# Emitting three sequence mixers step by step between the K steps of the projections, and gating a head ahead of its norm

## The chip, the cores and the metric

The kernel runs on one core of one Trainium2 chip, as one program. The metric is the device time of an execution in microseconds (us); the numbers given are a median of three runs and one further execution that the hardware profiler recorded. The engines are TensorE (PE in the rows, its weight loads PEld), VectorE (DVE), ScalarE (ACT), GpSimd (POOL) and the queue that issues most DMAs (SP). Each engine works through its own instructions in order.

## The reference, cut to what matters

A 1024 x 1024 sequence passes through two blocks of two layers. The change touches the first block alone, whose layer is:

```
h    = rms_norm(x, pre_gain) * (1 + scale) + shift       # scale, shift, gate: mods of c
proj = h @ w_in                                          # 13 column groups
a = sliding_window_attention(aq, ak, av, sinks) * silu(ag)              # 8 heads of 64
r = rms_norm(retention(rq, rk, rv)) * silu(rg)                          # 4 heads of 64
g = rms_norm(gated_linear_attention(gq, gk, gv, log_a), gain) * silu(gg)  # 4 heads of 64
x = x + gate * rms_norm(concat(a, r, g) @ w_out, post_gain)
```

The norm of `r` and `g` is taken over each head's 64 values, so it does not matter for the result whether the product with silu comes before or after the multiplication by the norm's factor, as long as the factor is computed from the values without silu.

## The kernel before, in words

Rows (tokens) are handled in groups of four tiles of 128 (`GT = 4`), two groups (g) per layer (l), four steps in the first block. A step of `block1` does, in this order of emission: `p_attn` (products for keys and values, queries, and the attention gate, each 8 K steps), `finish` of the step before (`out_product`: the product with w_out, 2 x 8 K steps), `s_attn` (the attention mixer), `p_ret` (two products), `s_ret` (the retention mixer), `p_gla` (two products, with the norm and transposes of the next step's input between them), `s_gla` (the gated linear attention mixer). Every fp32 product is split in a high and a low part: `split_weights` makes `wh` on ACT (L201) and `wl` on DVE (L202) from each 128 x 512 weight tile, and `product` issues three matmuls (L489) per output tile and K step, 12 in a K step of four tiles, into the four PSUM banks `mm`.

What the mixers use beside `mm`: two PSUM banks `sm` for scores and transposes, and a single bank `o` for the sum over values. That bank is shared by the attention, the retention, the gated linear attention and `mods_acc.close` (L282), which reduces a chunk of the modulation vectors. Five SBUF buffers `sc` hold the mixers' temporaries. `aside` advances the modulation vectors by one chunk (8 weight tiles `aw`, DVE L310, ACT L315, POOL L316).

A retention or gated head ends in `head_norm`: ACT squares the bank `o` (L798), DVE sums the squares of each head (L800), POOL makes the factor (`rsqrt`, L207 and L208), DVE multiplies the bank by the factor (L803), POOL multiplies by the gate `sg` (L805), and `into` transposes the result on TensorE (L510) and splits it into the tiles `M` that `finish` reads. `s_gla` works in 14 levels (two halves `u` of seven block sizes `s`): POOL differences (L943, L944), ACT exponential (L945), DVE products (L947, L949), two matmuls (L954), DVE predicated copy (L957); after all 14 come the four tiles' values and norms.

What sets the order: the code is recorded by a tile framework, whose scheduler builds each engine's order by itself, by priority (order of emission, weight splits and evictions ahead) and its own cost model. A mixer emitted before a product thus does not run before it as a whole: the product's matmuls fill the places where the mixer's next instruction is not ready by that model.

Of the kernel before, what the change touches and what calls it, by code (L numbers as in the profile page):

```python
# [162 lines left out]
class Net:  # L163
    HP, HE, HX = 3000, 800, 600

    def __init__(self, ctx, tc, a):
        self.tc, self.nc, self.a = tc, tc.nc, a
        self.ctx = ctx
        self.n = 0
        self.pools = {}  # L170
# [250 lines left out]

    def split_weights(self, hi, lo, raw, g):
# [31 lines left out]
    def product(self, lhs, wsrc, nk, ncol, form, evac, gains=None, also=None):  # L454
# [18 lines left out]
        for k in range(nk):  # L473
# [8 lines left out]
            for get, w, outs, acc, flags, _ in sets:  # L482
                H, Lo = get(k)
                for j in range(outs):
                    for n, (x, y) in enumerate(((H, wh), (H, wl), (Lo, wh))):
# [5 lines left out]
                        else:  # L491
                            m = min(P, ncol - j * P)
                            nc.tensor.matmul(acc[j][:m, :w], lhsT=y[:, j * P:j * P + m], rhs=x[:, :w],  # L493
                                             start=first, stop=last)
        with self.tc.high_priority(self.HE):
# [197 lines left out]
    def s_attn(self, l, g, st, mT):  # L693
# [51 lines left out]
        def close(t):  # L745
# [11 lines left out]
            self.into(mT, 0, t, a, 4)  # L757
# [36 lines left out]

    def head_norm(self, O, sg, mT, k0, t):
        nc = self.nc
        sq = self.T("sc", [P, 256])
# [4 lines left out]
        y = self.T("sc", [P, 256])  # L802
        nc.vector.tensor_tensor(y.rearrange("p (h d) -> p h d", d=64), O[:, :256].rearrange("p (h d) -> p h d", d=64),  # L803
                                r.unsqueeze(2).to_broadcast([P, 4, 64]), ALU.mult)
        nc.gpsimd.tensor_tensor(y, y, sg, ALU.mult)  # L805
        self.into(mT, k0, t, y, 2)

    def s_ret(self, l, g, st, mT):
# [7 lines left out]
        for t in range(GT):  # L816
            tb = g * GT + t
            sc = self.T("sc", [P, 2, 2, P])
            dm = self.k1("dmask").rearrange("p (a b i) -> p a b i", a=2, b=2)
            for b in range(2):  # L820
# [4 lines left out]
                nc.vector.tensor_tensor(sc[:, :, b, :], sp, dm[:, :, b, :], ALU.mult)  # L825
            O = self.T("o", [P, 512])
            old, new = state[tb % 2], state[(tb + 1) % 2]
            if tb > 0:
                qd = self.T("sc", [P, 2, P])
                nc.vector.tensor_tensor(qd, rqk[t][:, 0:2, :], self.k1("qdec").rearrange("p (a i) -> p a i", a=2), ALU.mult)  # L830
# [15 lines left out]
            self.head_norm(O, sg[t], mT, 4, t)  # L846
            if t % 2:
                self.aside()

# [46 lines left out]
    def s_gla(self, l, g, st, mT):  # L896
# [20 lines left out]
        nc.vector.tensor_mul(kx, kx, k)  # L917
        kt = self.T("gq", [P, GT, P])
        self.transposes(kt, kx, 4)
        pr = self.T("sc", [P, 512])  # L920
        nc.vector.tensor_mul(pr, q, k)
# [5 lines left out]
        SC = []  # L927
        for u in range(2):
            us = slice(u * 256, u * 256 + 256)
            sc = self.T("st", [P, 8, P])  # L930
            SC.append(sc)
            nc.gpsimd.tensor_tensor(sc, self.k1("ident").unsqueeze(1).to_broadcast([P, 8, P]),
                                    dg[:, u * 8:u * 8 + 8].unsqueeze(2).to_broadcast([P, 8, P]), ALU.mult)
            qb = self.T("st", [P, 4, 256])
            for h in range(4):
                nc.scalar.activation(qb[:, h, :], q[:, us], AF.Copy, scale=self.k1("hsel")[:, h:h + 1])
            for n, s in enumerate((64, 32, 16, 8, 4, 2, 1)):
                v = b[:, us].rearrange("p (n two s) -> p n two s", two=2, s=s)
                nb = 256 // (2 * s)
                e = self.T("sc", [P, 256])  # L940
                ev = e.rearrange("p (n two s) -> p n two s", two=2, s=s)
                ref = v[:, :, 0, s - 1:s].to_broadcast([P, nb, s])
                nc.gpsimd.tensor_tensor(ev[:, :, 0, :], ref, v[:, :, 0, :], ALU.subtract)  # L943
                nc.gpsimd.tensor_tensor(ev[:, :, 1, :], v[:, :, 1, :], ref, ALU.subtract)  # L944
                nc.scalar.activation(e, e, AF.Exp, scale=I16)  # L945
                kl = self.T("sc", [P, 256])
                nc.vector.tensor_mul(kl, k[:, us], e)  # L947
                ql = self.T("sc", [P, 4, P])
                nc.vector.tensor_tensor(ql.rearrange("p h (n s) -> p h n s", s=s),  # L949
                                        qb.rearrange("p h (n two s) -> p h n two s", two=2, s=s)[:, :, :, 1, :],  # L950
                                        ev[:, :, 1, :].unsqueeze(1).to_broadcast([P, 4, nb, s]), ALU.mult)
                lp = self.T("sm", [P, 8, 64])
                for t in range(2):
                    nc.tensor.matmul(lp[:, t * 4:t * 4 + 4, :], lhsT=kl[:, t * P:(t + 1) * P],  # L954
                                     rhs=ql[:, :, t * 64:t * 64 + 64], start=True, stop=True)
                nbb = P // (2 * s)
                nc.vector.copy_predicated(  # L957
                    sc.rearrange("p th (n two s) -> p th n two s", two=2, s=s)[:, :, :, 1, :],
                    self.lm[:, n * 64:(n + 1) * 64].rearrange("p (n s) -> p n s", s=s).unsqueeze(1).to_broadcast([P, 8, nbb, s]),
                    lp.rearrange("p th (n s) -> p th n s", s=s))  # L960
                if n in (1, 4):
                    self.aside()
        for t in range(GT):
# [17 lines left out]
            if t % 2:  # L981
                self.aside()
# [682 lines left out]
```

## Time and profile before

| | us |
|---|---|
| median of 3 runs (lowest, highest) | 3988.06 (3983.03, 3991.77) |
| the profiled execution, its own time | 3987.53 |
| its span, first to last instruction | 3985.8 |
| TensorE busy in the span | 3756.6 (94%) |
| VectorE busy | 2432.5 (61%) |
| ScalarE busy | 1691.2 (42%) |
| GpSimd busy | 678.9 (17%) |

The first block takes roughly the first 1290 us of the span. A busy share is an average over stages; matmuls are pipelined, so a busy TensorE can still lose time between two starts, and an idle engine costs nothing where another one sets the end. The granted clock of TensorE over the span is 0.978 of full speed.

### The profile page before, as it was taken

Reading aid. Unit: us, or ns where it says so; the run is one execution under the profiler, and the core shown is the slowest. Engines: PE = TensorE matmul, PEld = TensorE weight load, DVE = VectorE, ACT = ScalarE, POOL = GpSimd, SP = SyncE. Lnnn points to the kernel's source line nnn. Section 1 sums busy time; section 2 is a strip of 40 time slices with the busy share of each in tenths; the row PEclk is TensorE's granted clock in tenths of the full one; section 3 lists DMA queues with packets and bytes.
Section 4 is the critical chain, followed back from the end, with each engine's and each line's share of the span. In section 5 each row is a group of like instructions: output and inputs, shape, how many; then the busy total and the mean of one; then the engine's idle time right before and its main releaser. Section 6 shows DMA issues by size and latency. Waiting matters only on the chain. (4 is left out here: it accounts for less than half of the span.)

```text
span 3985.8 us, 55585 instructions
## 1 busy us (share of the span) xinstructions
PE 3756.6 (94%) x19144; PEld 3068.2 (77%) x19144; DVE 2432.5 (61%) x5177; ACT 1691.2 (42%) x3652; POOL 678.9 (17%) x1058
## 2 busy tenths in 40 slices
PE   7999988998999999999999899999899999999998
PEld 5777776776777787777788788888787788887886
DVE  7677678678667657576545744344766554455444
ACT  4433344454444545455334422224544443344333
POOL 2121145235333212221001100000312100001000
PEclk9999999999999999999999999999999999999999
DMA  6234333333422412432433542222422113335332
GB/s 213 73 117 123 123 114 112 127 113 102 132 89 78 138 42 71 143 107 76 153 101 101 188 131 74 64 64 91 136 64 85 68 61 97 96 97 168 96 97 94
DMA packets 249453, 420.38 MB, mean 105 GB/s; under 512 B 32001, under 2 KB 101202, under 8 KB 249170
## 3 DMA queue, kind: packets, MB, share of 16 engines
q1 hardware_dynamic: 241426, 389.52, 31.5%
q0 software_dynamic: 7744, 27.30, 1.8%
q8 instruction: 151, 2.47, 0.3%
q14 instruction: 132, 1.08, 0.1%
HBM read 389.42 MB, written 27.30 MB: 105 GB/s over the span
## 5 line engine op out<-in xcount | busy, mean ns | idle before, releaser
L202 DVE TENSOR_TENSOR wl<-wr,wh 128x512 fp32r<-128x512 f32 (+2 forms) x948 | 640.6, 677 | 799.4 <-ACT wh L201 796.0
L201 ACT CAST wh<-wr 128x512 fp32r<-128x512 f32 (+2 forms) x948 | 554.2, 586 | 1235.8 <-PE mm L489 524.0
L489 PE MATMUL mm<-wh,M 128*128 128x512 f32 (+1 forms) x2944 | 955.3, 396 | 28.3 <-ACT M L201 17.4
L489 PE MATMUL mm<-wh,H 128*128 128x512 f32 (+2 forms) x2432 | 785.3, 396 | 7.7 <-DVE pe L640 3.6
L493 PE MATMUL mm<-H,wh 128*128 128x512 f32 x2240 | 725.6, 395 | 1.5 <-ACT wh L201 1.5
L489 PEld LDWEIGHTS mm<-wh,M 128*128 128x128 f32 x2944 | 553.0, 191 | 146.8 <-ACT M L201 25.9
L489 PE MATMUL mm<-wl,M 128*128 128x512 f32 (+1 forms) x1472 | 577.3, 392 | 0.4 <-DVE wl L202 0.4
L489 PEld LDWEIGHTS mm<-wh,H 128*128 128x128 f32 x2432 | 451.6, 194 | 95.0 <-ACT aw L315 3.3
L493 PEld LDWEIGHTS mm<-H,wh 128*128 128x128 f32 x2240 | 418.6, 189 | 80.6 <-ACT wh L201 1.8
L489 PE MATMUL mm<-wl,H 128*128 128x512 f32 (+2 forms) x1216 | 478.2, 393 | 0.0
L493 PE MATMUL mm<-H,wl 128*128 128x512 f32 x1120 | 444.1, 396 | 0.0
L489 PEld LDWEIGHTS mm<-wl,M 128*128 128x128 f32 x1472 | 281.5, 191 | 49.9 <-DVE wl L202 1.0
L489 PEld LDWEIGHTS mm<-wl,H 128*128 128x128 f32 x1216 | 235.5, 194 | 38.0 <-DVE wl L202 0.4
L493 PEld LDWEIGHTS mm<-H,wl 128*128 128x128 f32 x1120 | 211.7, 189 | 37.8
L1333 PEld LDWEIGHTS o<-kv,pT 128*128 128x128 f32 x1280 | 159.7, 193 | 28.6 <-ACT pT L1329 21.4
L1333 PE MATMUL o<-kv,pT 128*128 128x64 f32 x1280 | 169.0, 275 | 4.9 <-DVE pT L1327 2.9
L316 POOL TENSOR_TENSOR ac<-ac,aw 128x256 f32<-128x256 f32 x168 | 140.4, 836 | 157.4 <-ACT aw L315 140.5
L310 DVE SCALAR_TENSOR_TENSOR ac<-aw,c,ac 128x256 f32<-128x256 f32 x280 | 159.7, 570 | 8.3 <-DMA aw<-in_w_mod 4.4
L1418 DVE TENSOR_TENSOR Z<-Z,mm 128x512 f32<-128x512 f32 x224 | 140.1, 680 | 2.5 <-PE mm L489 2.1
L544 POOL TENSOR_TENSOR tm<-tm 128x1 f32<-128x1 f32 x34 | 7.0, 207 | 735.9 <-ACT pe L539 735.6
L1310 DVE CUSTOM_DVE_ANT_0 p<-sm,c,c 128x384 f32<-128x384 f32 (+1 forms) x144 | 82.0, 570 | 76.3 <-PE sm L1308 74.6
L1316 ACT ACTIVATE p<-p,ti 128x640 f32<-128x640 f32 (+2 forms) x144 | 110.8, 770 | 40.9 <-DVE ti L1315 38.0
(353 smaller groups left out, 5746.4 us busy)
## 6 DMA issues: line engine op xcount, KB each, us to landing
wr<-in_w_ff SPq DMA_DIRECT2D x512, 256.0 KB, 2.7
wr<-in_w_in SPq DMA_DIRECT2D x240, 256.0 KB, 2.7
wr<-in_w_out SPq DMA_DIRECT2D x144, 256.0 KB, 2.7
x<-xd SPq DMA_DIRECT2D x64, 512.0 KB, 4.9
aw<-in_w_ada SPq DMA_DIRECT2D x192, 128.0 KB, 2.1
x<-in_w_ada SPq DMA_DIRECT2D x96, 256.0 KB, 3.0
xd<-x POOLq DMA_DIRECT2D x44, 512.0 KB, 3.7
wr<-in_w_in SPq DMA_DIRECT2D x152, 128.0 KB, 2.1
```

What stands on the lines that cost most here:

```text
L201: self.nc.scalar.copy(hi, src)
L202: self.nc.vector.tensor_sub(lo, src, hi.bitcast(F32))
L310: nc.vector.scalar_tensor_tensor(acc[:, 0], wt, c[0], acc[:, 0], ALU.mult, ALU.add)
L316: nc.gpsimd.tensor_tensor(acc[:, 1], acc[:, 1], wt, ALU.add)
L489: nc.tensor.matmul(acc[j][:, :ncol], lhsT=x[:, j * P:(j + 1) * P], rhs=y[:, :ncol], start=first, stop=last)
L493: nc.tensor.matmul(acc[j][:m, :w], lhsT=y[:, j * P:j * P + m], rhs=x[:, :w], start=first, stop=last)
L544: nc.gpsimd.tensor_tensor(ss[j][:, 0:1], ss[j][:, 0:1], ss[j][:, 1:2], ALU.add)
L1310: nc.vector.tensor_tensor_reduce(sc[:, at:at + w], ps[:, :w], mask, 1.0, prev, ALU.add, ALU.max, accum_out=acc)
L1316: nc.scalar.activation(sc[:, :at], sc[:, :at], AF.Exp, bias=nm, accum_out=den[:, h:h + 1])
L1333: nc.tensor.matmul(O[:, h * 64:h * 64 + 64], lhsT=pT[:, i, :], rhs=Vs(j)[:, sl], start=i == 0, stop=i == nk - 1)
L1418: nc.vector.tensor_add(y, y, ps)
```

## The change

The three mixers become generators. `product` calls `tick` after each K step, and a tick runs the oldest generator up to its next `yield`. `s_attn` and `s_ret` are thus emitted between the K steps of `p_ret` and `p_gla`, and `s_gla` between those of the next step's `p_attn`, after which `drain` runs what is left, ahead of `finish`. Within a mixer, the scores of a unit, the values of the one before and the transposes into `M` of one still earlier are in different steps. `head_norm` multiplies the bank `o` by the gate on DVE first, and then by the factor in SBUF on DVE; POOL's gate is gone. The retention's score tile moves from `sc` to `st`. In `s_gla` the values of the first two tiles come with the tenth and the twelfth level, not after the fourteenth. `s_attn` calls `aside` twice instead of four times per step, the other mixers as often as before.

```diff
+    def tick(self):
+        while self.bg:
+            if next(self.bg[0], self) is not self:
+                return
+            self.bg.pop(0)
...
@@ product, at the end of each K step
+            self.tick()
...
@@ s_attn
-        scores(*units[0])
-        for i, (t, e) in enumerate(units):
-            if i + 1 < len(units):
-                scores(*units[i + 1])
-            values(t, e)
-            if e:
-                close(t)
-            if e:
-                self.aside()
+        ready = []
+        for i in range(len(units) + 1):
+            if i < len(units):
+                scores(*units[i])
+                yield True
+            if i:
+                values(*units[i - 1])
+                t, e = units[i - 1]
+                if e:
+                    ready.append((t, close(t)))
+                elif ready:
+                    self.into(mT, 0, ready[0][0], ready.pop(0)[1], 4)
+                yield True
+                if i % 4 == 3:
+                    self.aside()
...
@@ head_norm
+        y = self.T("sc", [P, 256])
+        nc.vector.tensor_tensor(y, O[:, :256], sg, ALU.mult)
         sq = self.T("sc", [P, 256])
         nc.scalar.activation(sq, O[:, :256], AF.Square)
...
         r = self.rsqrt(ss, 4, 4.0 / 64, 4 * EPS)
-        y = self.T("sc", [P, 256])
-        nc.vector.tensor_tensor(y.rearrange("p (h d) -> p h d", d=64), O[:, :256].rearrange("p (h d) -> p h d", d=64),
-                                r.unsqueeze(2).to_broadcast([P, 4, 64]), ALU.mult)
-        nc.gpsimd.tensor_tensor(y, y, sg, ALU.mult)
-        self.into(mT, k0, t, y, 2)
+        yh = y.rearrange("p (h d) -> p h d", d=64)
+        nc.vector.tensor_tensor(yh, yh, r.unsqueeze(2).to_broadcast([P, 4, 64]), ALU.mult)
+        return y
...
@@ s_ret
+        for i in range(GT + 2):
+            if i > 1:
+                self.into(mT, 4, i - 2, y[i - 2], 2)
+            if 0 < i <= GT:
+                y[i - 1] = values(i - 1, *sc[i - 1])
+            if i < GT:
+                sc[i] = scores(i)
+            yield True
+            if i in (2, 4):
                 self.aside()
+                yield True
...
@@ s_gla
+        for i in range(len(units) + 1):
+            if i:
+                scores(*units[i - 1], *made)
+            if i < len(units):
+                made = level(*units[i])
+            if i in (9, 11):
+                y[i // 2 - 4] = values(i // 2 - 4)
+            if i in (11, 13):
+                self.into(mT, 6, i // 2 - 5, y[i // 2 - 5], 2)
+            yield True
+            if i % 7 in (2, 5):
+                self.aside()
+        for i in range(2, GT + 2):
+            if i < GT:
+                y[i] = values(i)
+            if i > 3:
+                self.into(mT, 6, i - 2, y[i - 2], 2)
+            yield True
+            if i in (2, 4):
                 self.aside()
...
@@ block1
                 self.p_attn(l, g, hT, st, tables if n == 0 else None)
+                self.drain()
                 if pend:
                     finish(*pend)
                 mT = self.pair(GT, "M")
-                self.s_attn(l, g, st, mT)
+                self.bg.append(self.s_attn(l, g, st, mT))
                 self.p_ret(l, g, hT, st)
-                self.s_ret(l, g, st, mT)
+                self.bg.append(self.s_ret(l, g, st, mT))
...
                 self.p_gla(l, g, hT, st, ahead)
-                self.s_gla(l, g, st, mT)
+                self.bg.append(self.s_gla(l, g, st, mT))
```

How the built order changes is shown at three places; a row is a line of the program, the operation, what it writes and reads (with its buffer's number), the size, and a repetition.

The first place is TensorE at the last retention head of the second step. `o` is the bank of the head, `pu` its values, `sc` in the transposes' row (L510 before, L524 in the changed kernel) the normed and gated head, `mm` a product's bank. Before:

```order
L834 MATMUL o_5147<-pu_4956,sc_5138 128x64 x3
L489 MATMUL mm_5446<-wh_5556,H_2341 128x512
L489 MATMUL mm_5447<-wh_5556,H_2340 128x512
L489 MATMUL mm_5447<-wl_5557,H_2340 128x512
L489 MATMUL mm_5447<-wh_5556,H_2341 128x512
L489 MATMUL mm_5444<-wh_5574,H_2342 128x512
L489 MATMUL mm_5444<-wl_5575,H_2342 128x512
L489 MATMUL mm_5444<-wh_5574,H_2343 128x512
L489 MATMUL mm_5445<-wh_5574,H_2342 128x512
L489 MATMUL mm_5445<-wl_5575,H_2342 128x512
L510 MATMUL sm_5166<-c_76,sc_5163 128x128 x2
```

And in the changed kernel, its last rows before the transposes:

```order
L283 MATMUL o_5123<-c_76,ac_5000 128x1 x2
L502 MATMUL mm_5394<-wh_5455,H_2263 128x512
L398 MATMUL mt_5329<-c_76,x_5268 128x128
L398 MATMUL mt_5329<-c_76,x_5277 128x128
L398 MATMUL mt_5329<-c_76,x_5286 128x128
L398 MATMUL mt_5329<-c_76,x_5295 128x128
L502 MATMUL mm_5395<-wh_5455,H_2262 128x512
L502 MATMUL mm_5395<-wl_5456,H_2262 128x512
L502 MATMUL mm_5395<-wh_5455,H_2263 128x512
L524 MATMUL sm_5414<-c_76,sc_5101 128x128 x2
```

Before, 9 product matmuls stand between a head's values and its transposes. In the changed kernel these rows are preceded by 5 more product matmuls that follow the head's values (L862), so that 9 of them, 4 transposes of the next step's input and a chunk of the modulation stand between. Of the step's four retention heads it is the one with the fewest; the one before it has 22 product matmuls there.

The second place is DVE at the same head: `sc_5163` and `sc_5101` are the head's result, `o` its bank, `ti` sums and factor. Before:

```order
L800 TENSOR_REDUCE ti_5158<-sc_5156 128x4
L310 SCALAR_TENSOR_TENSOR ac_5058<-aw_5088,c_70,ac_5058 128x256
L803 TENSOR_TENSOR sc_5163<-o_5147,ti_5160 128x256
L202 TENSOR_TENSOR H_5369<-pe_5431,H_5368 128x512
L202 TENSOR_TENSOR wl_6254<-wr_6255,wh_6253 128x272
```

And in the changed kernel:

```order
L820 TENSOR_TENSOR sc_5101<-o_5094,pu_4834 128x256
L403 TENSOR_SCALAR pe_5325<-mt_5320,ab_5216,md_2702 128x512
L824 TENSOR_REDUCE ti_5105<-sc_5103 128x4
L286 TENSOR_TENSOR md_2702<-o_5123,c_78 128x2
L309 TENSOR_SCALAR ac_5127<-aw_5128,c_70 128x256
L827 TENSOR_TENSOR sc_5101<-sc_5101,ti_5107 128x256
```

DVE reads the bank `o` in its first instruction of the head (L820) where before it read it in its last (L803), and has one instruction more.

The third place is POOL in the first step's gated linear attention, at the last levels (L943 and L944 before, L983 and L984 in the changed kernel); `ti` is a head's sum and factor, `pu` a gate. Before:

```order
L944 TENSOR_TENSOR sc_2891<-gb_867 128x64x2
L943 TENSOR_TENSOR sc_2903<-gb_867 128x128
L944 TENSOR_TENSOR sc_2903<-gb_867 128x128
L207 TENSOR_SCALAR ti_2930<-ti_2928 128x4
L208 TENSOR_TENSOR ti_2930<-ti_2930,c_76 128x4
L805 TENSOR_TENSOR sc_2933<-sc_2933,pu_2565 128x256
L207 TENSOR_SCALAR ti_2957<-ti_2955 128x4
```

And in the changed kernel:

```order
L984 TENSOR_TENSOR sc_3113<-gb_867 128x16x8
L208 TENSOR_SCALAR ti_3058<-ti_3056 128x4
L209 TENSOR_TENSOR ti_3058<-ti_3058,c_76 128x4
L983 TENSOR_TENSOR sc_3143<-gb_867 128x32x4
L984 TENSOR_TENSOR sc_3143<-gb_867 128x32x4
L983 TENSOR_TENSOR sc_3200<-gb_867 128x64x2
L984 TENSOR_TENSOR sc_3200<-gb_867 128x64x2
L208 TENSOR_SCALAR ti_3169<-ti_3167 128x4
L209 TENSOR_TENSOR ti_3169<-ti_3169,c_76 128x4
L983 TENSOR_TENSOR sc_3259<-gb_867 128x128
```

The factors of two heads now stand between the differences of the last levels, and no gate stands on POOL.

## Rows read from the trace of the kernel before

**Rows 1.** Windows: stretch, length, busy (instructions) of PE, PEld, DVE, ACT, POOL; PEclk, DMA, GB/s.

```profile
40.00:1290.00 1250.00, 1158.10 (x6032) 933.66 (x6031) 916.71 (x2048) 560.82 (x1350) 380.11 (x530) 0.96 0.37 110
1290.00:3985.00 2695.00, 2579.85 (x13033) 2119.89 (x13031) 1492.37 (x3084) 1113.66 (x2276) 285.39 (x505) 0.99 0.31 100
```

**Rows 2.** Waits of PE, 90 to 1290 us: total, times, longest.

```profile
PE sm L510 <- POOL sc L805: 22.2, 17, 3.7
PE sm L954 <- DVE sc L949: 15.2, 13, 3.3
PE o L282 <- DVE ac L310: 7.3, 5, 3.2
PE o L969 <- DVE sc L803: 7.2, 8, 2.0
PE o L282 <- DVE sc L803: 6.1, 9, 1.3
PE sm L732 <- ACT sc L722: 6.1, 3, 2.5
```

**Rows 3.** Timeline of one head, 551 to 558 us: start, duration, engine, line, [idle before].

```profile
550.80 0.88 PE L834 MATMUL o<-pu,sc 128*128 128x64 f32 x6 [0.28 <-DVE sc L825]
...
552.06 0.39 ACT L798 ACTIVATE sc<-o 128x256 f32<-128x256 f32 x1 [1.05 <-POOL ac L316]
...
552.48 0.42 DVE L800 TENSOR_REDUCE ti<-sc 128x4 f32<-128x256 f32 x1 [1.11 <-ACT sc L798]
...
553.43 1.02 POOL L208 TENSOR_TENSOR ti<-ti,c 128x4 f32<-128x4 f32 x1
...
554.48 0.42 DVE L803 TENSOR_TENSOR sc<-o,ti 128x256 f32<-128x256 f32 x1 [1.19 <-POOL ti L208]
...
555.11 1.48 POOL L914 TENSOR_TENSOR sc<-gb 128x512 f32<-128x512 f32 x1
...
556.55 0.92 POOL L805 TENSOR_TENSOR sc<-sc,pu 128x256 f32<-128x256 f32 x1
...
557.53 0.44 PE L510 MATMUL sm<-c,sc 128*128 128x128 f32 x2 [3.70 <-POOL sc L805]
```

**Rows 4.** Windows of 40 us around stalls and at a product alone; columns as in rows 1.

```profile
560.00:600.00 40.00, 36.31 (x198) 31.71 (x197) 31.83 (x70) 24.49 (x62) 19.06 (x23) 0.85 0.41 116
600.00:640.00 40.00, 34.95 (x163) 25.86 (x163) 37.08 (x87) 18.87 (x38) 21.63 (x31) 1.00 0.34 100
640.00:680.00 40.00, 34.40 (x169) 27.92 (x167) 32.20 (x67) 19.10 (x41) 19.54 (x28) 0.97 0.35 106
...
1160.00:1200.00 40.00, 35.59 (x151) 27.05 (x150) 18.22 (x44) 9.99 (x24) 11.51 (x17) 0.74 0.21 70
1280.00:1320.00 40.00, 40.00 (x204) 32.79 (x203) 23.71 (x56) 18.72 (x44) 1.35 (x3) 1.00 0.43 129
```

**Rows 5.** Timeline of PE in a product alone, 370 to 376 us.

```profile
371.68 0.39 PE L489 MATMUL mm<-wl,M 128*128 128x512 f32 x1
371.91 0.62 PE L489 MATMUL mm<-wh,M 128*128 128x512 f32 x2
372.36 0.39 PE L489 MATMUL mm<-wl,M 128*128 128x512 f32 x1
```

**Rows 6.** Timeline of PE in the first attention, 124 to 126 us.

```profile
124.44 1.00 PE L741 MATMUL o<-kv,sc 128*128 128x64 f32 x8
125.37 0.82 PE L712 MATMUL sm<-kv,pt 64*128 64x128 f32 x5
```

**Rows 7.** Groups by line, 90 to 1290 us: busy, mean ns, idle before, releasers.

```profile
L310 DVE SCALAR_TENSOR_TENSOR ac<-aw,c,ac 128x256 f32<-128x256 f32 x273 | 156.3, 573 | 8.3 <-DMA aw<-in_w_mod 4.4 <-DMA aw<-in_w_ada 1.8
...
L957 DVE COPY_PREDICATED st<-c,sm 128x512 f32<-128x512 uint8 x56 | 49.8, 889 | 6.5 <-PE sm L954 6.2
...
L949 DVE TENSOR_TENSOR sc<-st,sc 128x512 f32<-128x512 f32 x56 | 41.6, 744 | 0.0
...
L947 DVE TENSOR_TENSOR sc<-pt,sc 128x256 f32<-128x256 f32 x56 | 28.8, 514 | 7.6 <-ACT sc L945 7.6
...
L803 DVE TENSOR_TENSOR sc<-o,ti 128x256 f32<-128x256 f32 x32 | 13.6, 424 | 23.1 <-POOL ti L208 22.7
```

**Rows 8.** Wait of POOL for a head's sum, 90 to 1290 us.

```profile
POOL ti L207 <- DVE ti L800: 130.7, 28, 13.4
```

More of the change, by code (lines that the diff above doesn't have):

```diff
@@ L169, in __init__ @@
         self.n = 0
+        self.bg = []
         self.pools = {}
@@ L419, in norm_T, with drain @@
         return get, nt
+    def tick(self):
[3 more added lines that the diff above has]
+            self.bg.pop(0)
+    def drain(self):
+        while self.bg:
+            self.tick()
     def split_weights(self, hi, lo, raw, g):
@@ L815, in s_ret, with scores @@
         state = st["rstate"]
-        for t in range(GT):
+        def scores(t):
             tb = g * GT + t
-            sc = self.T("sc", [P, 2, 2, P])
+            sc = self.T("st", [P, 2, 2, P])
             dm = self.k1("dmask").rearrange("p (a b i) -> p a b i", a=2, b=2)
@@ L825, in s_ret, with values @@
                 nc.vector.tensor_tensor(sc[:, :, b, :], sp, dm[:, :, b, :], ALU.mult)
+            qd = None
+            if tb > 0:
+                qd = self.T("sc", [P, 2, P])
+                nc.vector.tensor_tensor(qd, rqk[t][:, 0:2, :], self.k1("qdec").rearrange("p (a i) -> p a i", a=2), ALU.mult)
+            return sc, qd
+        def values(t, sc, qd):
+            tb = g * GT + t
             O = self.T("o", [P, 512])
@@ L926, in s_gla, with level @@
         nc.vector.tensor_copy(dg, dp)
-        SC = []
-        for u in range(2):
+        SC, QB = [], []
+        def level(u, n, s):
             us = slice(u * 256, u * 256 + 256)
[L930 to L962, printed above, removed]
@@ L963, in s_gla @@
-        for t in range(GT):
+            if n == 0:
+                SC.append(self.T("st", [P, 8, P]))
+                nc.gpsimd.tensor_tensor(SC[u], self.k1("ident").unsqueeze(1).to_broadcast([P, 8, P]),
+                                        dg[:, u * 8:u * 8 + 8].unsqueeze(2).to_broadcast([P, 8, P]), ALU.mult)
+                QB.append(self.T("st", [P, 4, 256]))
+                for h in range(4):
+                    nc.scalar.activation(QB[u][:, h, :], q[:, us], AF.Copy, scale=self.k1("hsel")[:, h:h + 1])
@@ new lines, in level, with scores @@
+            kl = self.T("sc", [P, 256])
+            nc.vector.tensor_mul(kl, k[:, us], e)
+            ql = self.T("sc", [P, 4, P])
+            nc.vector.tensor_tensor(ql.rearrange("p h (n s) -> p h n s", s=s),
+                                    QB[u].rearrange("p h (n two s) -> p h n two s", two=2, s=s)[:, :, :, 1, :],
+                                    ev[:, :, 1, :].unsqueeze(1).to_broadcast([P, 4, nb, s]), ALU.mult)
+            return kl, ql
+        def scores(u, n, s, kl, ql):
+            lp = self.T("sm", [P, 8, 64])
+            for t in range(2):
+                nc.tensor.matmul(lp[:, t * 4:t * 4 + 4, :], lhsT=kl[:, t * P:(t + 1) * P],
+                                 rhs=ql[:, :, t * 64:t * 64 + 64], start=True, stop=True)
+            nbb = P // (2 * s)
+            nc.vector.copy_predicated(
+                SC[u].rearrange("p th (n two s) -> p th n two s", two=2, s=s)[:, :, :, 1, :],
+                self.lm[:, n * 64:(n + 1) * 64].rearrange("p (n s) -> p n s", s=s).unsqueeze(1).to_broadcast([P, 8, nbb, s]),
+                lp.rearrange("p th (n s) -> p th n s", s=s))
@@ L964, in s_gla, with values @@
+        def values(t):
             tb = g * GT + t
```

32 lines of the change are left out of this document (22 added, 10 removed).

## The prediction

> **What bounds the kernel now.** I read the windows first, to find what part of the span the change can touch. The first block is the first 1290 us; in 40 to 1290 us TensorE is busy 1158.1 of 1250 us and idle 91.9, DVE is busy 917, and the granted clock is 0.96 [rows 1]. The second block keeps its code, so it is not costed. TensorE is the bound, and what the change can win is those 91.9 us and what the clock costs. The clock has two levels, 1.2 and 2.4 GHz, so a mean of 0.96 says that 8% of 1250 us, 100 us, ran at the lower one; work done there takes twice as long, so at most 50 us are lost by it. The floor for any such change is thus 3988 - 92 - 50 = 3846 us.
>
> Then I read who TensorE waits for there [rows 2]. Three kinds of wait belong to what the change rewrites: the transposes of a finished head wait for POOL's gate (22.2 us in 17 waits), the next user of bank `o` waits for DVE's last read of it (7.2 + 6.1 us), and the levels of the gated attention wait for DVE's products (15.2 us). The wait for modulation chunks (7.3 us) and for the softmax (6.1 us) stay.
>
> The timeline shows one head [rows 3]. Its values end at 551.68 us, the gate on POOL at 557.47: 5.8 us in series through five instructions on three engines. Of these the gate is 0.92 us, and 1.65 us pass between DVE's multiply (end 554.90) and its start, most of it behind a 1.48 us subtraction of the next mixer on POOL. On TensorE the 9 product matmuls that follow cover 9 x 0.227 = 2.0 us (three take 0.68 us [rows 5]), and then it stands for 3.7 us. The clock answers such waits: the window right behind this one has 0.85, one later with TensorE busy 35.6 of 40 us has 0.74, while a product by itself is busy throughout at 1.00 [rows 4].
>
> **The change, part by part.**
>
> *Head chain.* The same head without the POOL gate and its queue is 5.8 - 0.92 - 1.65 = 3.2 us, plus a DVE multiply from the bank in front of it. Its nearest row is L803, same size, same bank, 424 ns [rows 7], so about 3.7 us here; a head that did not queue behind a subtraction needs about 5.3. What TensorE has to do meanwhile I counted in the two built orders. Product matmuls between a head's values and its transposes: median 13 to 16 before, 19 to 21 in the change. With the scores, transposes and modulation passes between counted too, at 0.116 us a pass (8 in 0.93 us [rows 6]), the median cover goes from about 4.1 to 5.9 us, and 9 of 32 heads stay under 4.9. I take 7 of the 22.2 us as left: -15 us (bounds 0 and -22).
>
> In the trace before, ACT's Square and DVE's multiply of bank `o` are 2 us apart [rows 3]; in the built order of the change the Square waits for the gate, which is why 0.42 us stand in series above. The Trainium skill (PSUM — Partial Sum Buffer, section "PSUM bank collisions raise a hardware error") says that no two of TensorE, ScalarE and VectorE may be in one bank's partitions at once, reads included, which speaks against a gate and a Square on one bank; no row of the trace before shows it. Were the two side by side, the term would be -17 and the sum 2 us better.
>
> *Bank `o`.* Before, it is released at the end of L803, 3.2 us after the values; in the change after the gate and the Square, 0.42 + 0.39 us plus the hops between, some 1.1 us. The 17 waits for it are 0.8 us long on average and at most 2.0 [rows 2], and 2.1 us are gained: -11 of 13.3 us (bounds 0 and -13).
>
> *Levels.* A level costs DVE 0.51 + 0.74 + 0.89 = 2.15 us [rows 7], ahead of which come POOL and ACT. Between the first and the last level of a step the order has 186, 193, 155 and 85 product matmuls before, and 204, 230, 206 and 131 in the change: a fifth more cover. I take a third of 15.2 us: -5 (bounds 0 and -15).
>
> *Clock.* Fewer waits of 2 to 4 us should leave fewer stretches at the lower level. Of the lost time of at most 50 us I take a good third, about the share of the removed waits (31 of 91.9): -18 (bounds +5 and -40).
>
> *What is added.* DVE gets 32 gates, 32 x 0.424 = 13.6 us. The retention heads' half lies beside products; the gated attention's lies where DVE is busy 37.1 of 40 us [rows 4], so I put +5 on the path (bounds 0 and 13.6). POOL loses 32 gates, which nothing waits for but the transposes.
>
> POOL's queue gets a new order: in each step two heads' factors stand between the differences of the last levels, and the differences behind them wait until PE, DVE and ACT have made that head's sum. The nearest row is POOL's present wait for a head's sum, 130.7 us in 28, 4.7 us each [rows 8]. Behind it now stand levels, whose scores TensorE waits for. There are 8 such heads; the order leaves mostly 12 to 25 product matmuls between the scores of the last levels, 3 to 6 us of cover, so I take +4 (bounds 0 and 8 x 4.7 = 37.6).
>
> The modulation vectors come in 10 chunks per step and not in 12. The second layer's need 17 calls before the second step's `ahead`; 18 were made before, 14 are now, so three chunks are made at one go between the two products of `p_gla`: 24 x 0.573 = 13.8 us of DVE [rows 7], beside a product of 96 matmuls, 21.8 us. I take +3 (bounds 0 and 13.8). Their 24 weight tiles, and those of the later chunks, stay on SP among as many weight loads as before; TensorE waits for a weight in no row worth naming there, so this costs nothing while three loaded weight tiles stand ahead; without that cover a 128 KB load would show as a wait for `wh`.
>
> The retention's scores in `st` instead of `sc`, the second gating multiply in SBUF instead of PSUM, and the attention's start (a few steps later, inside `p_ret`) are costed at nothing: TensorE's work is the same, and products lie beside them.
>
> Sum: -15 - 11 - 5 - 18 + 5 + 4 + 3 = **-37 us**. The profiled execution took 3987.5 us, which gives 3950.5; the median of the runs is 0.5 us higher: **3951 us**.
>
> **The rivals.**
>
> *Everything closes.* All waits of rows 2 but the modulation's go (22.2 + 15.2 + 13.3 + 6.1 = 56.8 us) and the clock with them (40 us), less the added 12: 3988 - 85 = 3903 us. For it: the long waits are few, and the clock falls behind them. Against: DVE is nearly full in the gated attention, so its levels can't all come in time.
>
> *The change doesn't do what it says.* The scheduler mixed mixers and products before: up to the last level both orders go 784 times from a product to something else or back. Then only the head's own shorter chain and its bank count, a half of -26, eaten by DVE's 13.6: 3988 us, within 5. For it: both orders come from the same scheduler with the same model of durations, and that model's errors, not the emission, make the waits. Against: the cover behind heads did grow in the order.
>
> *POOL's queue turns on the levels* (slower). The in-order POOL holds the differences of the next level behind a factor that waits for its sum, 4.7 us for each of 8 heads, and TensorE reaches the next scores first: +37.6 instead of +4, and the clock falls behind those waits, +5 instead of -18: -15 - 11 - 5 + 5 + 5 + 37.6 + 3 = +20, 4008 us. It decides when the wait is longer than the cover of the next level, 3 to 6 us; at half of the heads the sum is still near 3975. For it: rows 8. Against: the wait now lasts so long mostly because POOL has nothing before it to do.
>
> **How the numbers follow.** About 0.2% (8 us) is what a measurement of this kernel can tell from no change. The forecast, 3930 to 3975 us, has 0.53; everything closes (3900 to 3930) 0.17; no change (3980 to 3996) 0.14; slower (from 3996) 0.16. Faster: 0.53 + 0.17 = 0.70; same 0.14; slower 0.16. The range from 3908 to 3996 leaves out the lower part of the first rival and the whole slower one, some 0.2.
>
> **What would show it.** Right: the transposes' wait for a head falls under 8 us in total, and names DVE instead of POOL; waits for bank `o` fall under 4 us; the first block's clock rises to 0.97 or more; the block ends 30 to 45 us earlier and the second block takes as long as before. Wrong: the waits of L954's successor on DVE or POOL grow over 20 us (POOL's queue); or DVE is busy over 38 of 40 us in windows where TensorE is idle; or idle time of TensorE falls and the clock doesn't rise, which takes 18 us off the gain.

## The result and the profile after

| | before | changed |
|---|---|---|
| median, us (lowest, highest, runs) | 3986.48 (3983.03, 3991.77, 4) | 3935.84 (3926.94, 3939.9, 4) |
| ratio, 95% interval | | 0.9869 [0.9848, 0.9889] |
| profiled execution, its span, us | 3985.8 | 3935.3 |
| granted clock over the span | 0.978 | 0.986 |

The change gains 51 us where 37 were forecast (the median before is that of four executions here). The time lies inside the range, 15 us below the forecast.

First the windows of the changed kernel (columns as in [rows 1]). The first block is cut at 1240 us, since its span is 50.5 us shorter and the stretch behind has the same length as before:

```profile
40.00:1240.00 1200.00, 1129.57 (x6055) 914.06 (x6053) 927.36 (x2078) 558.63 (x1359) 353.46 (x499) 0.99 0.38 115
1240.00:3935.00 2695.00, 2576.82 (x13010) 2115.31 (x13010) 1494.74 (x3085) 1111.10 (x2269) 282.85 (x505) 0.98 0.32 100
```

Against [rows 1] the second block is the same (TensorE 2576.8 and 2579.9 us of 2695), so all of the gain is in the first. There TensorE's idle time falls from 91.9 to 1200 - 1129.6 = 70.4 us, and its busy time from 1158.1 to 1129.6 us. A busy time can fall for the same matmuls because those at 1.2 GHz count as busy longer: in the kernel before, three product matmuls took 1.28 us from start to start where the granted clock was 0.51 (1190 to 1200 us), and 0.68 at full speed [rows 5]:

```profile
1197.51 0.63 PE L489 MATMUL mm<-wl,H 128*128 128x512 f32 x1
1198.79 0.63 PE L489 MATMUL mm<-wl,H 128*128 128x512 f32 x1
```

So of 50 us in these windows, 21.5 are idle time and 28.5 the clock. The later window holds 23 matmuls more, since its cut falls a little further on in the work. Over the whole span, where each trace holds the same 19,144 matmuls, the blur is gone. The page of the changed kernel has

```profile
PE 3726.1 (95%) x19144; PEld 3045.4 (77%) x19144; DVE 2445.6 (62%) x5209; ACT 1685.8 (43%) x3652; POOL 649.3 (17%) x1026
```

so idle time falls from 3985.8 - 3756.6 = 229.2 to 3935.3 - 3726.1 = 209.2 us, by 20.0, and busy time by 30.5. The granted clocks agree: 0.978 of 3985.8 us leaves (1 - 0.978) x 3985.8 = 88 us lost to the lower level, 0.986 of 3935.3 us 55, so 33 us.

Then TensorE's waits from 90 to 1250 us (total, times, longest), to set beside [rows 2]. L524 is the transposes (L510 before), L997 a level's scores (L954), L1014 the values of the gated attention (L972), L283 a modulation chunk (L282), L746 the softmax's transposes (L732):

```profile
PE sm L997 <- DVE sc L989: 19.6, 22, 2.4
PE sm L524 <- DVE sc L827: 12.4, 10, 1.9
PE o L1014 <- DVE st L1000: 6.0, 6, 2.2
PE mm L502 <- DVE pe L654: 3.6, 4, 2.5
PE sm L746 <- ACT sc L736: 3.0, 4, 1.1
...
PE o L283 <- DVE ac L311: 1.7, 3, 1.2
PE o L283 <- POOL ac L317: 1.2, 2, 0.6
...
PE o L283 <- ACT sc L822: 0.2, 1, 0.2
```

The head's wait falls by 9.8 us and names DVE. Both waits for bank `o` behind a head, 13.3 us, are gone but for 0.2. The levels wait 4.4 us longer than before, and the values behind the last level's store 6.0 us, where it was 0.9. And no wait is as long as the longest before: 3.7 us (heads), 3.3 (levels) and 3.2 (chunks) have become 1.9, 2.4 and 1.2.

One head, from its gate to its transposes (start, duration, engine, line, idle before):

```profile
339.72 0.42 DVE L820 TENSOR_TENSOR sc<-o,pu 128x256 f32<-128x256 f32 x1
340.06 0.48 DVE L311 SCALAR_TENSOR_TENSOR ac<-aw,c,ac 128x256 f32<-128x256 f32 x1
340.18 0.39 ACT L822 ACTIVATE sc<-o 128x256 f32<-128x256 f32 x1
340.45 0.69 DVE L203 TENSOR_TENSOR wl<-wr,wh 128x512 fp32r<-128x512 f32 x1
341.05 0.48 DVE L311 SCALAR_TENSOR_TENSOR ac<-aw,c,ac 128x256 f32<-128x256 f32 x1
341.45 0.41 DVE L824 TENSOR_REDUCE ti<-sc 128x4 f32<-128x256 f32 x1
...
341.95 0.36 POOL L208 TENSOR_SCALAR ti<-ti 128x4 f32<-128x4 f32 x1 [3.96 <-DVE ti L824]
...
342.39 1.01 POOL L209 TENSOR_TENSOR ti<-ti,c 128x4 f32<-128x4 f32 x1
...
343.43 0.42 DVE L827 TENSOR_TENSOR sc<-sc,ti 128x256 f32<-128x256 f32 x1 [1.18 <-POOL ti L209]
...
343.91 0.44 PE L524 MATMUL sm<-c,sc 128*128 128x128 f32 x2 [1.44 <-DVE sc L827]
```

The gate's start to the multiply's end takes 4.1 us (the median of the 32 heads is 4.2, and four take over 7), where the forecast had 3.7 for the whole chain. 0.9 us of it is DVE's queue: the Square ends at 340.57, and a weight split and a modulation accumulation stand ahead of the reduction. POOL's two steps are 1.45 us from start to end, with nothing ahead of them. The Square (340.18) starts behind the gate (end 340.14), as the built order has it, and in all 32 heads it starts at least 0.03 us behind the gate's end. ACT stands 31.7 us for the gate in all:

```profile
L822 ACT ACTIVATE sc<-o 128x256 f32<-128x256 f32 x32 | 12.2, 381 | 39.1 <-DVE sc L820 31.7 <-PE mt L398 7.3
```

By the rule of the Trainium skill that the prediction weighed (PSUM — Partial Sum Buffer, section "PSUM bank collisions raise a hardware error") they have to be in series, and the trace agrees; it doesn't show what would happen without the order.

### The profile page after: what moved, and what is told of

It reads as the page before. It is cut to its first block, busy times and chain, and to the rows that moved or that the text cites. A ratio compares the mean times of both kernels' runs of the same rounds, so it can differ in the third digit from the quotient of the medians.

```text
span 3935.3 us, 55613 instructions
## 1 busy us (share of the span) xinstructions
PE 3726.1 (95%) x19144; PEld 3045.4 (77%) x19144; DVE 2445.6 (62%) x5209; ACT 1685.8 (43%) x3652; POOL 649.3 (17%) x1026
```

## The experiments

"Lost" is (1 - granted clock) x span of the profiled execution, the most that the lower clock can cost. "Idle" is that span less TensorE's busy time. Every trace holds the same 19,144 matmuls, and span - idle - lost is 3662 to 3675 us in all of them, so these two columns account for a span to some 10 us. "Waits" adds TensorE's waits of the heads, of the levels, and of the values behind the last level's store (12.4 + 19.6 + 6.0 for the change), 90 to 1250 us, to 1290 for the kernel before, g1 and g2. The runs g1 to g4 stood beside a before of 3987.55 us, h1 to h4 beside 3986.24, i1 to i3 beside 3985.97.

The granted clock is on record for every execution, not only for the profiled one. "Rest" is the range of time - lost over all of a kernel's executions, an estimate of its time without the lower clock.

| run | median us (lowest, highest) | ratio [95%] | lost us | idle us | waits us | rest us |
|---|---|---|---|---|---|---|
| kernel before | 3986.48 (3983.03, 3991.77) | | 88 | 229.2 | 38.3 | 3886 to 3902 |
| changed kernel | 3935.84 (3926.94, 3939.9) | 0.9869 [0.9848, 0.9889] | 55 | 209.2 | 38.0 | 3876 to 3882 |
| g1_gate_only | 3961.5 (3956.34, 3967.58) | 0.9935 [0.9923, 0.9947] | 71 | 221.6 | 38.0 | 3884 to 3892 |
| g2_steps_old_norm | 3960.44 (3958.73, 3970.72) | 0.9937 [0.9926, 0.9949] | 55 | 230.0 | 37.9 | 3896 to 3906 |
| g3_no_ticks | 3958.6 (3948.62, 3966.47) | 0.9926 [0.9912, 0.9939] | 71 | 211.4 | 29.9 | 3879 to 3885 |
| g4_gla_whole | 3942.09 (3936.09, 3945.67) | 0.9886 [0.9873, 0.9899] | 59 | 206.6 | 31.4 | 3874 to 3884 |
| h1_values_last | 3937.97 (3932.76, 3940.7) | 0.988 [0.9867, 0.9892] | 63 | 209.2 | 31.3 | 3874 to 3882 |
| h2_aside12 | 3934.0 (3931.39, 3938.61) | 0.9871 [0.9856, 0.9886] | 67 | 201.7 | 34.4 | 3865 to 3869 |
| h3_into_later | 3947.56 (3938.42, 3949.1) | 0.99 [0.9886, 0.9914] | 67 | 217.5 | 28.1 | 3880 to 3883 |
| h4_levels_two_ahead | 3950.85 (3940.6, 3960.19) | 0.9909 [0.9893, 0.9925] | 63 | 213.5 | 32.2 | 3875 to 3885 |
| i1_chunks_out_of_gla | 3924.46 (3920.19, 3928.23) | 0.9845 [0.9832, 0.9859] | 55 | 200.7 | 25.8 | 3861 to 3870 |
| i2_chunks_out_into_later | 3927.34 (3924.28, 3934.96) | 0.9856 [0.9842, 0.987] | 63 | 200.8 | 20.5 | 3862 to 3872 |
| i3_levels_stored_twice | 3950.59 (3945.13, 3950.99) | 0.9908 [0.9895, 0.9922] | 75 | 211.8 | 45.4 | 3876 to 3882 |

Two things limit the column "lost". The second block, whose code is the same everywhere, has 32 to 46 us of it in the thirteen traces. And one kernel loses a different amount each time: h4_levels_two_ahead 55 to 83 us over its six executions, of which the profiled one is among the two shortest. So differences of some 10 us in it decide nothing alone; the column "rest" is the steadier one. By it, g3, g4, h1, h3, h4 and i3 are all equal to the change within a few us, and what sets the slower ones of them apart is the clock.

### The two halves, each by itself

The gate alone, in the kernel before:

```diff
 @@ head_norm
+    y = self.T("sc", [P, 256])
+    nc.vector.tensor_tensor(y, O[:, :256], sg, ALU.mult)
...
-    y = self.T("sc", [P, 256])
-    nc.vector.tensor_tensor(y.rearrange("p (h d) -> p h d", d=64), O[:, :256].rearrange("p (h d) -> p h d", d=64),
-                            r.unsqueeze(2).to_broadcast([P, 4, 64]), ALU.mult)
-    nc.gpsimd.tensor_tensor(y, y, sg, ALU.mult)
+    yh = y.rearrange("p (h d) -> p h d", d=64)
+    nc.vector.tensor_tensor(yh, yh, r.unsqueeze(2).to_broadcast([P, 4, 64]), ALU.mult)
```

> The kernel before with nothing but the new head_norm (gate on DVE from the bank first, then the factor in SBUF; no gate on POOL); the mixers are emitted whole, as before. My theory (shorter chain and an early bank are one half, the cover from stepping the other): the transposes' wait for a head falls from 22 to about 12 us, the waits for bank o from 13 to about 2, the clock of the first block rises from 0.96 to about 0.97, and the time is 3957 to 3967 us, about half of the change's gain of 51. Rival 1 (the gate is all of it): 3936 to 3942. Rival 2 (the stepping is all of it): 3980 to 3990.

The steps alone: the changed kernel with the old `head_norm` arithmetic (the same lines, the other way round).

> The changed kernel with the old head_norm: factor times bank on DVE, then the gate on POOL; all stepping stays. My theory: the transposes' wait is 10 to 14 us and names POOL, the waits for bank o are back at 8 to 13 us, and the time is 3955 to 3967. Rival 1 (gate is all): 3980 to 3990. Rival 2 (stepping is all): 3934 to 3942.

Measured: 26 us and 27 us faster, where both together, the change, are 51, so the halves add up. TensorE's waits of the gate alone (90 to 1290 us; L805 is there DVE's last multiply):

```profile
PE sm L510 <- DVE sc L805: 20.3, 21, 2.0
PE sm L954 <- DVE sc L949: 17.0, 19, 3.4
```

And of the steps alone (90 to 1290 us; L827 is there POOL's gate, L825 DVE's multiply from the bank):

```profile
PE sm L524 <- POOL sc L827: 17.5, 12, 2.3
PE sm L997 <- DVE sc L989: 17.2, 18, 1.6
PE o L283 <- DVE sc L825: 11.2, 12, 1.5
```

The gate alone hardly changes the sum of the heads' waits (20.3 for 22.2 us, where 12 were expected). It cuts the longest from 3.7 to 2.0 us and clears the waits for bank `o` behind a head but for 1.8 of 13.3 us. By the windows (TensorE busy 1142.1 of the 1226 us from 40 to 1266) idle time falls by 8 us only, from 91.9 to 83.9, while the loss to the lower clock falls from 88 to 71. The steps alone keep the waits for the bank and for POOL's gate, and cut their length too; the loss falls to 55. Their idle time doesn't fall at all (230.0 us for 229.2, and the rest 3896 to 3906 for 3886 to 3902): all of their 27 us is the clock. So each half gets most of its gain from the clock, not from less waiting. With both, the loss is no lower than with the steps alone (55), and what the gate takes off on top is idle time (209.2 for 230.0 us). That the steps alone gain 27 us is the end of the rival by which the change doesn't do what it says.

### What of the steps counts

> The changed kernel in which each mixer is emitted whole at the place where it is started, so that no K step of a product stands between its steps; the new order of the steps inside a mixer and the new head_norm stay. My theory (the cover is made by the K steps between): 3955 to 3967, as with the gate alone, with a head's transposes close behind its values again. Rival 3 (what helps is the new order inside the mixers, and the scheduler fills in products by itself either way): 3934 to 3944.

```diff
                 self.bg.append(self.s_attn(l, g, st, mT))
+                self.drain()
```

(the same behind `s_ret` and `s_gla`: the mixers keep their new inner order and the new gate, but are emitted in one piece)

> The changed kernel in which only the gated attention is emitted whole, right after its products; attention and retention stay stepped. The trace of the change shows no gain at the levels (19.6 us waited for DVE where it was 15.2). My theory: stepping the gated attention is worth little, 3936 to 3946, with level waits of 13 to 20 us. Rival (stepping it gains as much as the other two mixers together): 3950 to 3960.

The edit of the second run has the added line behind `s_gla` alone. Measured: without any tick 3958.6 us, 3 us from the gate alone and not to be told from it, so the inner order is worth little and the emission between the K steps some 23 us. Hardly any of the 23 is idle time (211.4 us for 209.2); the loss is 71 for 55 (over all executions 63 to 87, for 51 to 59). With only the gated attention in one piece, 3942.09: stepping that mixer is worth 6 us of the 23 at most (the intervals overlap), the attention and the retention the rest.

### The two costs of the sum, POOL's queue and the burst

```diff
@@ s_gla (h1_values_last)
-            if i in (9, 11):
-                y[i // 2 - 4] = values(i // 2 - 4)
-            if i in (11, 13):
-                self.into(mT, 6, i // 2 - 5, y[i // 2 - 5], 2)
...
-        for i in range(2, GT + 2):
+        for i in range(GT + 2):
...
-            if i > 3:
+            if i > 1:
@@ s_attn (h2_aside12)
-                if i % 4 == 3:
+                if i % 2 == 0:
                     self.aside()
```

> The changed kernel with the values of all four tiles of the gated attention after its fourteenth level, so that no head's factor stands on POOL between the differences of two levels. If POOL's queue holds the levels up (the slower rival of the prediction, its part of the waits of L997, 19.6 us where it was 15.2, and 6.0 us of L1014): level waits fall to 13 to 16 us, the time by 4 to 10 us against the change, to 3926 to 3932. If it doesn't: level waits 17 to 21 us, the four heads bunch at the end, and the time is the same or up to 8 us longer, 3936 to 3944.

> The changed kernel with four modulation chunks in each attention as before the change (12 per step, not 10; the three chunks at one go before the second layer's first norm are gone). The prediction put +3 us on this. If right: 3931 to 3936. If the chunks beside attention cost more than the burst: 3937 to 3946.

Measured: 3937.97 and 3934.0 us, beside 3935.84 of the change: neither can be told from it. No factor stands between the levels' differences in the first of these kernels, it isn't faster, and its levels wait as long as the change's (19.9 us for 19.6), so POOL's queue costs nothing measurable; that rival falls:

```profile
PE sm L997 <- DVE sc L989: 19.9, 18, 2.8
```

The second has 7.5 us less idle time than the change, and more loss, which leaves its time the same. In the changed kernel POOL's wait for a head's sum is still there, and TensorE's waits that name POOL, 90 to 1250 us, come to 1.2 us in the rows above:

```profile
POOL ti L208 <- DVE ti L824: 118.1, 26, 20.9
```

### Two ways to give the waiting chains more room

```diff
@@ s_ret; the two last heads of s_gla likewise (h3_into_later)
-        for i in range(GT + 2):
-            if i > 1:
-                self.into(mT, 4, i - 2, y[i - 2], 2)
+        for i in range(GT + 3):
+            if i > 2:
+                self.into(mT, 4, i - 3, y[i - 3], 2)
```

> The changed kernel with the transposes of a retention head, and of the gated attention's last two heads, one K step later still (12 more product matmuls, 2.7 us, between a head's values and its transposes). In the change 10 waits for a head's factor are left, 12.4 us. My theory (TensorE's wait is chain minus cover, and the clock follows the waits): the waits fall to 0 to 4 us, the lower clock in the first block shrinks further, and the time falls by 8 to 16 us to 3920 to 3930. Rival (what is left is set by DVE's load, so that a wait removed comes back at the next consumer): 3934 to 3942.

In the other, a level's products are made two K steps ahead of its scores and not one, with `ql` in `ys`:

> The changed kernel with a level's scores two K steps behind its products on DVE, not one (the queries' products take the buffers ys, which lie idle then, so that sc has room; the values move one step later with them). Waits of L997 are 19.6 us in 22 now. My theory (cover again): they fall to 4 to 8 us, and the time by 10 to 20 us to 3916 to 3928. Rival (DVE is full there, 37 of 40 us, so that the levels are bound by its work and not by the distance): waits stay 15 to 20 us, 3932 to 3940.

Both missed: 12 and 15 us slower than the change (the interval of the first touches the change's, 0.9886 for 0.9889). TensorE's waits of h3_into_later, 90 to 1250 us:

```profile
PE sm L997 <- DVE sc L989: 18.6, 20, 1.7
PE mm L502 <- DVE pe L654: 8.2, 4, 4.1
PE sm L524 <- DVE sc L827: 6.7, 6, 2.1
PE sm L746 <- ACT sc L736: 4.8, 4, 2.6
PE o L283 <- DVE ac L311: 4.4, 3, 2.2
```

and of h4_levels_two_ahead:

```profile
PE sm L997 <- DVE ys L989: 17.4, 12, 2.8
PE sm L524 <- DVE sc L827: 14.1, 10, 3.4
PE sm L524 <- DVE st L1000: 9.1, 4, 3.9
```

The heads' wait did fall in the first, from 12.4 to 6.7 us, as expected. It came back elsewhere, 4.6 us of it as a wait of the products for a bank that DVE hadn't emptied (8.2 for 3.6), with one of 4.1 us. The windows of the gated attention (columns as in [rows 1]), first of h3_into_later and then of the change, show the rest as clock:

```profile
540.00:660.00 120.00, 104.71 (x492) 84.79 (x491) 100.78 (x228) 57.48 (x127) 54.49 (x79) 0.91 0.41 123
840.00:960.00 120.00, 103.95 (x527) 85.34 (x526) 98.35 (x230) 60.76 (x140) 58.21 (x76) 0.94 0.37 114
```

```profile
540.00:660.00 120.00, 102.82 (x518) 81.51 (x517) 106.62 (x237) 59.62 (x134) 59.19 (x83) 0.99 0.45 132
840.00:960.00 120.00, 107.12 (x542) 85.43 (x543) 103.23 (x229) 61.69 (x135) 57.89 (x78) 0.99 0.38 111
```

Over these two windows the loss is (0.09 + 0.06) x 120 = 18 us against 2.4. In the second run the levels' waits got fewer and longer, and the heads' transposes wait 9.1 us for a level's store, where it was 1.1. Idle time as a whole didn't fall in either (217.5 and 213.5 us for 209.2). One thing fits both: in these windows of the change DVE is busy 106.6 and 103.2 of 120 us, so a wait that one consumer no longer has is met by the next one in DVE's queue. That was the theory for the last three runs.

### Is DVE's queue the bound in the gated attention?

```diff
@@ s_gla
             yield True
-            if i % 7 in (2, 5):
-                self.aside()
...
-            if i in (2, 4):
-                self.aside()
@@ s_attn
-                if i % 4 == 3:
+                if i % 2 == 0:
                     self.aside()
@@ block1
                 if pend:
+                    self.bg.append(self.asides())
                     finish(*pend)
+                    self.drain()
```

The new generator `asides` makes six chunks, one in every other K step of `finish`. The second run has the later transposes of the retention heads on top.

> Edit: the changed kernel with the modulation chunks of the gated attention's generator moved out of it: four instead of two in an attention stage, two in a retention stage as before, and six during the K steps of the output product, which runs with no mixer beside it. A chunk is 0.34 + 7 x 0.608 = 4.6 us of VectorE, so about 24 x 4.6 = 110 us of VectorE leave four stretches (240 to 350, 540 to 660, 840 to 960, 1130 to 1250 us of the changed kernel) in which VectorE is busy 409 of 470 us and TensorE idles 51 us. Theory A (in these stretches VectorE's queue as a whole is the bound, so that a wait taken away in one place comes back in another, which would also explain why the later transposes and the deeper levels did not help): the three waits on VectorE there (levels 19.6, heads' transposes 12.4, values on the level's store 6.0) fall by at least half together, time 3905 to 3922 us. Theory B (each wait is its own chain's latency, and VectorE's load does not matter): the three stay above 30 us together, time 3930 to 3942 us.

> Edit: the previous kernel (modulation chunks out of the gated attention) with the retention heads' transposes one K step later. Theory A: with VectorE relieved, a longer slot is worth what it was expected to be before: the heads' waits fall below 5 us and the time is 3 to 10 us under the previous kernel's. Theory B: as the previous kernel or up to 10 us slower, since the later transposes alone cost some 12 us in the changed kernel.

The third has the masked store of a level in a loop of two:

```diff
@@ scores of s_gla
-            nc.vector.copy_predicated(
+            for _ in range(2):
+                nc.vector.copy_predicated(
```

> Edit: the changed kernel with each level's masked store (the copy_predicated of 128x512, 0.887 us on VectorE) done twice, with the same result; 56 x 0.887 = 50 us of VectorE are added in the four stretches and nothing else. Theory A (VectorE's queue bounds there): at least half of it shows, time 3960 to 3985 us, and the added waits are spread over TensorE's waits on VectorE. Theory B (VectorE has room, as the 87% busy share would have it): under 10 us, time 3936 to 3946 us.

With the chunks out, the time is 3924.46 us, 11 below the change, its longest run (3928.23) about as long as the shortest of the change (3926.94), though the intervals of the ratios overlap by 0.0011. It is the fastest version of this study. But its edit holds that of h2_aside12 (four chunks beside the attention), so h2's 3934.0 us is what the move out of the gated attention is to be set against: 10 us, and all of its executions are shorter than all of h2's. TensorE's waits, 90 to 1250 us:

```profile
PE sm L524 <- DVE sc L827: 12.4, 11, 1.9
PE sm L997 <- DVE sc L989: 12.0, 15, 2.7
PE o L283 <- DVE ac L311: 8.9, 10, 2.4
PE mt L524 <- DVE pe L656: 4.9, 2, 4.7
...
PE o L1014 <- DVE st L1000: 1.4, 3, 0.7
```

and the windows, of which the second is the product with w_out, where the chunks now are:

```profile
540.00:660.00 120.00, 114.10 (x575) 94.03 (x575) 90.17 (x204) 55.60 (x127) 36.86 (x57) 0.99 0.33 101
660.00:720.00 60.00, 53.60 (x239) 42.83 (x238) 39.74 (x71) 26.71 (x66) 29.28 (x42) 0.89 0.62 200
840.00:960.00 120.00, 107.77 (x541) 87.91 (x540) 93.58 (x209) 53.30 (x116) 41.57 (x60) 0.96 0.29 87
```

Neither theory holds alone. The waits of the levels and of the values fall from 25.6 us (21.0 in h2) to 13.4 with DVE's load: that part was its queue. The heads' wait stays at 12.4 us. Half of it is the retention's, whose stretches were not relieved (6.3 us in the change, 7.6 here); the gated attention's half falls only from 6.1 to 4.8, which fits a head's own chain. And the chunks' own close, which waited 1.7 us for DVE in the change, now waits 8.9. TensorE's idle time as a whole is that of h2 (200.7 and 201.7 us): the waits moved, as theory A has it, and the gain over h2 shows in the loss (55 for 67 us; over all executions 55 to 67, where h2 has 63 to 71). With the later transposes on top (i2) the heads' wait falls to 8.5, not below 5, and the closes wait 13.7 on DVE; the time, 3927.34, can't be told from i1's.

The third run puts a price on DVE's time: 50 us more of it in these four stretches cost 15 us, 0.3 us each, between the two theories. TensorE's waits there, 90 to 1250 us (L1001 is the store):

```profile
PE sm L997 <- DVE sc L989: 22.2, 21, 2.4
PE sm L524 <- DVE sc L827: 14.5, 10, 2.8
PE o L1015 <- DVE st L1001: 8.7, 7, 2.3
```

These three grew by 7.4 us, but TensorE's idle time as a whole by 2.6 (211.8 for 209.2); the granted clock fell from 0.986 to 0.981, 20 us more of loss by the profiled executions. Here too most comes by the clock.

## Why the prediction was right, and where it was not

*Sign and mechanism: right, but for what the clock follows.* The rivals fell by experiment as told above; "everything closes" (3903) fell with the 38.0 us of waits that are left. The sum of those waits, though, doesn't order the runs: it was 38.3 us before, and g3_no_ticks has 29.9 us and took 3958.6.

*Clock: the term that was mis-sized.* "Of the lost time of at most 50 us I take a good third, about the share of the removed waits: -18." It measured -30.5 by TensorE's busy time and -33 by the granted clocks, 12 to 15 us more, and the whole forecast was 14 too careful. The share of the removed waits was the wrong measure: the gate alone takes 8 us off the idle time, for which that share would give 8 / 91.9 x 50 = 4, and 17 off the loss; the steps alone take nothing off the idle time, and 33 off the loss. What the loss follows stays open. The length of the longest waits is one candidate. In the window of [rows 4] behind the head that waited 3.7 us the clock was 0.85; in the changed kernel the same stretch of the span has more idle time (5.1 us for 3.7) at 1.00:

```profile
560.00:600.00 40.00, 34.95 (x168) 27.05 (x168) 37.39 (x79) 25.25 (x60) 21.63 (x28) 1.00 0.46 140
```

No experiment changes length alone. h3_into_later, with a wait of 4.1 us and a loss of 67 us, points the same way. h2_aside12, with 67 us and no wait over 2.9 us, doesn't, and neither does i1_chunks_out_of_gla, with a wait of 4.7 us and a loss of 55. And the loss varies between executions of one kernel, whose order of instructions is the same.

*Idle time: right in sum, by terms that were not, which is luck.* Forecast -15 - 11 - 5 + 5 + 4 + 3 = -19, measured -20.0. Bank `o`: -13.1 for -11, right. Head chain: -9.8 for -15. "I take 7 of the 22.2 us as left" counted the cover by instructions, but took the chain without DVE's queue (0.9 us of it in the head above; and before, a head ran through six instructions, not five, since [rows 3] leaves out L207); 12.4 are left. Levels: +4.4, and 5.1 more for the values behind them, where "a fifth more cover" was to give -5. The cover is there (771 product matmuls for 619, a quarter more), but what is late is DVE, at 89% and 86% busy in the windows of 540 and 840 us, and the change put one more instruction per head on it. The step that failed is that cover was counted in TensorE's matmuls against the chain of one level, not against DVE's load of the stretch; for the levels i1_chunks_out_of_gla bears it out, for the heads it is only in part shown. Two waits that were to stay fell instead, the chunks' on DVE from 7.3 to 1.7 us and the softmax's from 6.1 to 3.0.

*The added costs.* Burst and POOL's queue, +3 and +4: nothing that can be measured in the time. DVE's gates, +5: no run has them alone; for the gated attention's 16 the price of the last run gives an estimate of 16 x 0.424 x 0.3 = 2 us.

*What would show it.* Bank waits under 4 us, clock at 0.97 or more, DVE named: right. The heads' wait under 8 us: no, 12.4. The block's end 30 to 45 us earlier: 50. DVE over 38 of 40 us where TensorE idles: not quite, 37.4 in the window above.

## What to carry to other kernels

In a kernel that TensorE bounds, account for a change twice, as idle time and as work at the lower clock. Here the second was the larger part (31 of 51 us), and the steps alone gained 27 us without taking any idle time away. Do it over several executions, since the same kernel lost 55 us in one and 83 in another. Cover behind a chain helps only while the engine that runs the chain has room: look at its busy share in that stretch first. Beside a DVE that was busy 86 to 89%, longer slots cost 12 and 15 us, and moving work out of the stretch that has no due time there (the modulation chunks) gained 10. Read a bank once, early, so that its next user doesn't wait for the end of a chain.

## What was not expected of the hardware

The factor's multiply has the same size in both kernels. Before it reads the bank `o` (first row, from before, L803); in the changed kernel both inputs are in SBUF (second row). The columns are the least, median and greatest duration in ns:

```profile
L803 DVE TENSOR_TENSOR sc<-o,ti x32: 411/424/425, 221.6 to 1264.6; 128x256 f32<-128x256 f32 x32
```

```profile
L827 DVE TENSOR_TENSOR sc<-sc,ti x32: 405/425/1260, 216.2 to 1218.0; 128x256 f32<-128x256 f32 x32
```

From the bank it always takes 0.42 us, in the 8 of 32 cases too that overlap an instruction of POOL. From SBUF 21 of the 32 do. The other 11 take 0.62 to 1.26 us, 0.83 on average, and each overlaps an instruction of POOL that reads SBUF. A twelfth overlaps one that only writes (L942, which sets a state to zero) and takes 0.42 us. The longest, on DVE and POOL in the changed kernel:

```profile
819.75 1.26 DVE L827 TENSOR_TENSOR sc<-sc,ti 128x256 f32<-128x256 f32 x1 [1.19 <-POOL ti L209]
```

```profile
819.69 1.04 POOL L953 TENSOR_TENSOR sc<-gb 128x512 f32<-128x512 f32 x1
```

It ends 0.28 us after POOL's subtraction, which began just before it. The Trainium skill (SBUF — State Buffer, section "SBUF: two separate sides") says that a VectorE instruction with two inputs in SBUF and a GpSimd instruction that reads SBUF shut each other out; the 11 and the 21 agree with it. So the multiply that the change moved from the bank to SBUF took 11 x (0.83 - 0.42) = 4.5 us more of DVE in all, which the prediction had at nothing.
